# Attention inside a decoder step: scores of a head pair in two stretches, softmax blocks of both heads turned at one step

## The chip, the cores and the metric

The kernel runs on 1 core of one Trainium2 chip. The metric is device time of one execution in microseconds (us); the median of 3 runs of the kernel before is 1062.48 us, the runs lie between 1062.13 and 1064.51 us.

## The reference, cut to what matters

The whole is one inference step of a two-layer decoder for a prompt of 512 tokens and 8 sample tokens. The change touches one part only: the prompt's attention in the even layer, 16 heads of 64 features.

```python
def dilated_attn_prompt(q, k, v, slopes):
    qf = q.astype(jnp.float32) * (Dh ** -0.5)
    ...
    for w, d in DIL_PATTERNS:                 # (128,1), (512,4), (2048,16)
        ...
        s = jnp.einsum('bnirhd,bnjrhd->bnrhij', qs, kk)
        bias = -slopes[:, None, None] * (dist * d).astype(jnp.float32)
        s = jnp.where(valid[None, :, None, None], s + bias, -jnp.inf)
        m = jnp.max(s, axis=-1, keepdims=True)
        p = jnp.exp(s - m)
        l = jnp.sum(p, axis=-1)
        o = jnp.einsum('bnrhij,bnjrhd->bnirhd', p, vv) / l
        ...
    return combine_patterns(outs, lses)
```

For 512 tokens the three patterns and their merging come to one causal softmax per head, with a bias table that holds the slopes and the logarithm of how many patterns see a pair of positions. So a head is: scores of 512 queries against the keys up to each query, softmax, and the weighted sum of v.

## The kernel before, in words

**Products.** Nearly all of TensorE's work is products of a weight tile with the modulated input `h0` (1024 features by 520 tokens). Each operand is cut into a high part in the reduced format and a low part, the rest; a product is high times high, high times low, low times high. One product has 8 steps `k`, and a step is 6 matmuls (3 pairs of operands, each in two halves of 256 and 264 columns), written by `mm3` into a tile `mm`. ScalarE (ACT) makes the high part of the weights of a later product (`w_hi`, tile `whi`), VectorE (DVE) the low part in two pieces (`w_lo`, tile `wlo`).

**Head pairs.** `head_pair(p)`, for p from 0 to 7, handles two heads: four products, v, k, gate and q. After each, ACT copies the product out of PSUM (the PSUM side memory of TensorE), and then `sample_z` has DVE copy the 8 sample columns of the same tile into `zs`. The attention work of pair p itself is laid between the product steps of the next pair (of the next stage for p = 7).

**Steps and queues.** What is laid between is set by `tick()`, called once behind every product step. `at(n, f)` runs f at n ticks from now, ahead of all else; `put(f, after=n)` runs f at the earliest n ticks from now, at most one such call per tick; `put_fill` fills ticks in which no `put` call is due; `put2` has a list of its own, served at even ticks. `Q0 = 5`: the ticks of the list in `head_pair` count from 5 ticks behind the q product. So the order on every engine is fixed when the program is written; each engine then works through its list in order and waits with semaphores.

**One pair's work.** `score(blocks)`: for each block of 128 queries 6 matmuls with 64 rows, the two heads in the upper and the lower half of the rows; blocks 0 and 1 together (256 columns each), block 2 (384 columns) and block 3 (512) apart. `soft`: DVE adds the bias and finds the minimum, ACT takes the exponential, `norm` scales. `turn(e, g)` (line 604) transposes the softmax blocks of head e in three groups g of 4, 3 and 3 blocks, into an `aux` tile; ACT copies it to a high part, DVE makes the low part one tick later (`lo_of`, line 146 as a helper's line). `v_out` (line 518) transposes v, ACT copies it twice (`vtm`, and the high part in tile `v`), DVE makes its low part. `weigh(e, jb)`, four for each head, is two matmuls with `v`, the high part first and then the low part; `weigh(0, 2)` is the first that uses group 2 of head 0. `q_rows` transposes the q columns of the samples (line 536). The sample tokens' own window scores (`window_scores`, `window_sums`) are four DVE instructions of 1.2 us for each pair. `ada_two` and `ada_two_fin` prepare the next layer's modulation after every second pair: 32 matmuls, then 4 transposes with a reduction and three small instructions on DVE. The `aux` tiles share four PSUM buffers, taken in turn.

Of the kernel before, what the change touches and what calls it, by code (L numbers as in the profile page):

```python
# [18 lines left out]
P = 128  # L19
D = 1024  # L20
KT = D // P
S = 512
NB = 8
T = S + NB
# [62 lines left out]
def hybrid_kernel(ctx: ExitStack, tc: tile.TileContext, a, o):  # L87
# [17 lines left out]
    def tt(n=T, dt=F32, p=P):  # L105
        n_made[0] += 1
        return tp.tile([p, 530], dt, name=f"t_{n_made[0]}", tag="t")[:, 0:n]
# [14 lines left out]
    def aux(shape):  # L122
        return mk(auxp, shape, F32, "aux")
# [60 lines left out]
    def at(dt, fn, *args):  # L184
        seqn[0] += 1
        heapq.heappush(timed, (now[0] + dt, seqn[0], fn, args))
# [5 lines left out]
    def put_fill(fn, *args, after=0):  # L192
        fill.append((now[0] + after, fn, args))
# [314 lines left out]
    qdr = dram.tile([KT, NB, P], F32, name="qdr")  # L508

    Q0 = 5  # L510

    def head_pair(p):
        st = {}

        def v_out(vf):
            pt = aux([P, 4, P])
            for i in range(4):
                nc.tensor.transpose(pt[:, i, :], vf[:, i * P:(i + 1) * P], ident)  # L518
            vtm = tt(S)
            act(vtm, flat(pt))  # L520
            at(1, load, wv[:, :, p * P:(p + 1) * P], p4(vtm))
            vhl = t4(dt=F32R).rearrange("p (a e l d) -> p a e l d", a=4, e=2, l=2)
            vte = vtm.rearrange("p (a e d) -> p a e d", a=4, e=2)
            act(vhl[:, :, :, 0, :], vte)
            at(2, lo_of, vhl[:, :, :, 1, :], vte, vhl[:, :, :, 0, :])
            st["v"] = vhl
# [15 lines left out]
        def window_load():  # L542
            kw = big().rearrange("p (t b d) -> p t b d", t=2, b=NB)
            c = a["cache_win_k"][0].rearrange("b s h d -> s b (h d)")[:, :, p * P:(p + 1) * P]
            load(kw[:, 0], c[896:1024])
            load(kw[0:96, 1], c[512:896].rearrange("(n s) b d -> n s b d", s=4)[:, 0])
            load(kw[96:128, 1], c[0:512].rearrange("(n s) b d -> n s b d", s=16)[:, 0])
            st["kw"] = kw
            ada_w[p] = ada_load(1, "ss", p)
            if p % 2:  # L550
                at(20, put_fill, ada_two, 1, "ss", p - 1, (ada_w[p - 1], ada_w[p]))

        def q_load():
            st["qb"] = t4().rearrange("p (b d) -> p b d", b=NB)
# [3 lines left out]

        def score(blocks):

            ss_ = [aux([P, S]) for _ in range(2)]
            for qb in blocks:
                N = max(H0, (qb + 1) * P)
                c0 = H0 if qb == 1 else 0
                for c, (x, y) in enumerate(((0, 0), (0, 1), (1, 0))):
                    for e in range(2):
                        r = slice(64 * e, 64 * e + 64)
                        mm(
                            ss_[e][:, c0:c0 + N], st["q"][x][r, qb * P:(qb + 1) * P], st["k"][y][r, 0:N],
                            c == 0, c == 2,  # L570
                        )
            for i, qb in enumerate(blocks):
                for e in range(2):
                    soft(e, qb, ss_[e][:, i * H0:])

        def soft(e, qb, s):
            if qb == 0:
                st["mn", e], st["ls", e] = mk(cp, [P, 4], F32, "mn", 4), mk(cp, [P, 4], F32, "ls", 4)
                st["E", e] = []
            n = (qb + 1) * P  # L580
            mn, ls = st["mn", e][:, qb:qb + 1], st["ls", e][:, qb:qb + 1]
            sb = tt(n)
            nc.vector.tensor_tensor_reduce(  # L583
                out=sb, in0=s[:, 0:n], in1=bt[e][:, S - n:S], scale=1.0, scalar=3e38, op0=ALU.add, op1=ALU.min,
                accum_out=mn,
            )
            st["E", e].append(sb)
            at(1, act, sb, sb, ACTF.Exp, mn, -1.0, ls)
            at(3, norm, e, qb)
# [8 lines left out]

        groups = (((0, 0), (1, 0), (2, 0), (3, 0)), ((1, 1), (2, 1), (3, 1)), ((3, 3), (2, 2), (3, 2)))

        def turn(e, g):
            ep = aux([P, S])
            for c, blk in enumerate(groups[g]):
                nc.tensor.transpose(ep[:, c * P:(c + 1) * P], st["E", e][blk[0]][:, blk[1] * P:(blk[1] + 1) * P], ident)  # L604
            n = len(groups[g]) * P
            if g < 2:
                st["T", e, g] = hilo_later(1, ep[:, 0:n], n)
            else:
                st["T", e, g] = hi, lo = T2[e]
                act(hi[:, P:S], ep[:, 0:n])  # L610
                at(1, lo_of, lo[:, P:S], ep[:, 0:n], hi[:, P:S])

        def weigh(e, jb):
            if jb == 0:
# [31 lines left out]
        vf = tt(S)  # L646
        act(p2(vf), vps[:, :, 0:H0])
        sample_z(0, 48 + p, vps)
        put_fill(v_out, vf, after=2)
        kps = ps01[1] if p == 0 else z_tile(0, 40 + p, h0)  # L650
        kf = tt(S)
        act(p2(kf), kps[:, :, 0:H0])
# [19 lines left out]
            sample_z(0, 32 + p, qps)  # L672

        at(1, q_lo)
        for blocks, n in (((0, 1), 0), ((2,), 3), ((3,), 5)):
            put(score, blocks, after=Q0 + n)
        for e, fn, ticks in (
            (0, turn, (11, 13, 15)), (1, turn, (12, 14, 17)), (0, weigh, (18, 19, 20, 21)), (1, weigh, (22, 23, 24, 26)),
        ):
            for i, n in enumerate(ticks):  # L680
                put(fn, e, i, after=Q0 + n)
        put_fill(q_rows, after=4)


    T2 = [(tr(S), tr(S)) for _ in range(2)]
# [743 lines left out]
```

## Time and profile before

| | |
|---|---|
| median of 3 runs | 1062.48 us |
| the profiled execution, its own time | 1062.29 us |
| its span | 1060.3 us |
| TensorE (PE) busy | 98% |
| VectorE (DVE) busy | 59% |
| ScalarE (ACT) busy | 46% |
| attention stage of the head pairs, about | 60 to 322 us |

The time of an execution is 2.0 us longer than its span, so what the span gains or loses is read as a change of the time. PE's matmuls are pipelined: busy time overlaps, so what a piece of work costs is read here from the starts of the instructions around it and not from busy times. Column 2 of a timeline row is the busy time of the row's instructions; where several like instructions are merged, the row gives their count.

### The profile page before, as it was taken

How to read it: one execution, taken by the hardware profiler on the slowest of the kernel's cores; microseconds unless marked ns; L12 is line 12 of the kernel's file. 1: busy time of each engine (PE TensorE's matmuls, PEld its weight loads, DVE VectorE, ACT ScalarE, POOL GpSimd, SP SyncE). 2: the span in 40 equal slices, each digit the busy share in tenths (PEclk: the TensorE clock that was granted, in tenths of full speed). 3: DMA queues.
4: the chain of work that ended last, by engine and by line, in shares of the span. 5: the costliest groups of instructions: out<-in, count | busy, mean ns of one | idle time of the engine just before them, and what ended most of it. 6: DMA issues, size and time to landing. Idle time of an engine off the chain costs nothing.

```text
span 1060.3 us, 21050 instructions
## 1 busy us (share of the span) xinstructions
PE 1036.2 (98%) x8682; PEld 991.1 (93%) x8682; DVE 623.1 (59%) x1470; ACT 489.1 (46%) x884; POOL 4.3 (0%) x33
## 2 busy tenths in 40 slices
PE   5999999999999999999999999999999999999996
PEld 3899999999989999999999998999999999999996
DVE  4666676766785444456344486665657576674443
ACT  5666567665654222224233474435444453333333
POOL 0000000000000000000000000000000000000000
PEclk9999999999999999999999999999999999999999
DMA  9576654666536636613744246363826423225322
GB/s 348 209 255 196 184 157 169 173 211 190 142 119 203 196 107 194 199 60 129 240 154 140 100 159 205 103 204 118 261 83 213 159 80 129 80 83 169 100 71 81
DMA packets 82175, 168.95 MB, mean 159 GB/s; under 512 B 7208, under 2 KB 47240, under 8 KB 79000
## 3 DMA queue, kind: packets, MB, share of 16 engines
q1 hardware_dynamic: 81792, 167.09, 48.9%
q8 instruction: 68, 1.11, 0.4%
q10 hardware_dynamic: 288, 0.52, 0.1%
q14 instruction: 27, 0.22, 0.1%
HBM read 149.40 MB, written 18.65 MB: 158 GB/s over the span
## 4 chain that ended last, share of the span: by engine, by line
PE 90%; DVE 5%; ACT 2%; issue 1%; DVEq 0%; ACTq 0%
PE mm L160 74%; PE aux L160 13%; DVE t L146 2%; PE aux L604 1%; ACT t L140 1%; DVE wlo L146 1%; DVE t L149 0%; PE aux L1299 0%; PE aux L518 0%; DVE big L149 0%; PE aux L973 0%; PE aux L980 0%; PE aux L374 0%; ACT md L140 0%; ACT whi L140 0%
## 5 line engine op out<-in xcount | busy, mean ns | idle before, releaser
L160 PE MATMUL mm<-t,whi 128*128 128x256 f32 (+1 forms) x4608 | 759.1, 286 | 1.1 <-DVE zs L143 0.8
L160 PEld LDWEIGHTS mm<-t,whi 128*128 128x128 f32 x4608 | 636.1, 188 | 19.9 <-issue 15.5
L160 PE MATMUL mm<-t,wlo 128*128 128x256 f32 (+2 forms) x2304 | 465.8, 282 | 0.0
L160 PEld LDWEIGHTS mm<-t,wlo 128*128 128x128 f32 x2304 | 358.1, 188 | 0.0
L146 DVE TENSOR_TENSOR wlo<-wraw,whi 128x512 fp32r<-128x512 f32 x288 | 188.4, 683 | 58.1 <-ACT whi L140 57.4
L140 ACT ACTIVATE whi<-wraw 128x1024 fp32r<-128x1024 f32 x144 | 151.6, 1053 | 94.3 <-PE mm L160 58.7
L146 DVE TENSOR_TENSOR t<-t,t 128x520 fp32r<-128x520 f32 (+6 forms) x182 | 119.0, 657 | 99.3 <-ACT t L140 97.7
L140 ACT ACTIVATE t<-t 128x520 fp32r<-128x520 f32 (+3 forms) x116 | 71.0, 616 | 161.8 <-DVE t L149 103.1
L140 ACT ACTIVATE t<-aux 128x512 f32<-128x512 f32 (+7 forms) x156 | 70.9, 464 | 133.3 <-PE aux L160 83.4
L140 ACT ACTIVATE t<-mm 128x512 f32<-128x512 f32 (+2 forms) x116 | 56.3, 507 | 111.3 <-PE mm L160 109.1
L146 DVE TENSOR_TENSOR t<-aux,t 128x384 fp32r<-128x384 f32 (+6 forms) x120 | 58.6, 494 | 42.8 <-ACT t L140 38.0
L160 PE MATMUL aux<-t,t 64*128 64x256 f32 (+6 forms) x384 | 54.0, 324 | 0.0
L160 PE MATMUL aux<-t,v 128*128 128x512 f32 (+2 forms) x224 | 50.0, 325 | 0.0
L160 PEld LDWEIGHTS aux<-t,t 64*128 64x128 f32 (+1 forms) x384 | 41.0, 186 | 4.3
L583 DVE CUSTOM_DVE_ANT_0 t<-aux,t 128x128 f32<-128x128 f32 (+3 forms) x64 | 28.2, 488 | 27.5 <-PE aux L160 27.5
L140 ACT ACT_TABLE_LOAD x32 | 41.1, 1283 | 1.3 <-PEq L1414 0.7
L140 ACT ACTIVATE t<-t,mn 128x128 f32<-128x128 f32 (+3 forms) x64 | 35.4, 554 | 7.9 <-DVE mn L583 7.9
L160 PEld LDWEIGHTS aux<-t,v 128*128 128x128 f32 x224 | 34.8, 188 | 1.8 <-DVE t L146 0.8
L149 DVE SCALAR_TENSOR_TENSOR big<-v,ksc,big 128x256 f32<-128x256 f32 x64 | 27.7, 480 | 11.8 <-ACT big L140 10.4
L143 DVE COPY zs<-mm 128x8 f32<-128x8 f32 x76 | 12.0, 158 | 37.2 <-ACT t L140 31.8
L146 DVE TENSOR_TENSOR t<-mm,t 128x512 f32<-128x512 f32 (+1 forms) x24 | 16.5, 689 | 29.2 <-PE mm L160 21.6
L146 DVE TENSOR_TENSOR gtmp<-mm,mG 128x8 f32<-128x8 f32 x16 | 2.6, 165 | 44.8 <-PE mm L160 44.8
(153 smaller groups left out, 557.7 us busy)
## 6 DMA issues: line engine op xcount, KB each, us to landing
wraw<-in_w_in_e SPq DMA_DIRECT2D x64, 512.0 KB, 4.9
wraw<-in_w_in_o SPq DMA_DIRECT2D x48, 512.0 KB, 3.7
big<-in_ada_e SPq DMA_DIRECT2D x12, 1024.0 KB, 11.8
big<-in_ada_o SPq DMA_DIRECT2D x12, 1024.0 KB, 9.8
wraw<-in_w_out_e SPq DMA_DIRECT2D x16, 512.0 KB, 3.9
big<-in_state_ret SPq DMA_DIRECT2D x16, 512.0 KB, 8.0
out_new_ret_sample<-big SPq DMA_DIRECT2D x16, 512.0 KB, 5.1
wraw<-in_w_out_o SPq DMA_DIRECT2D x16, 512.0 KB, 3.4
```

What stands on the lines that cost most here:

```text
L140: return nc.scalar.activation(out=out, in_=in_, func=func, scale=scale, **kw)
L143: return nc.vector.tensor_copy(out, in_)
L146: return nc.vector.tensor_tensor(out=out, in0=in0, in1=in1, op=op)
L149: return nc.vector.scalar_tensor_tensor(out=out, in0=in0, scalar=scalar, in1=in1, op0=op0, op1=op1)
L160: nc.tensor.matmul(out, lhsT=lhsT, rhs=rhs, start=start, stop=stop)
L583: nc.vector.tensor_tensor_reduce(out=sb, in0=s[:, 0:n], in1=bt[e][:, S - n:S], scale=1.0, scalar=3e38, op0=ALU.add, op1=ALU.min, accum_out=mn,
L604: nc.tensor.transpose(ep[:, c * P:(c + 1) * P], st["E", e][blk[0]][:, blk[1] * P:(blk[1] + 1) * P], ident)
```

## The change

The scores of blocks 2 and 3 form one stretch at tick Q0 + 4 (before: block 2 at Q0 + 3, block 3 at Q0 + 5), in four `aux` tiles, where block 2's two and block 3's two were asked for apart before. `q_rows` is called at the head of the first stretch of scores. `turns(g)` transposes group g of both heads at one tick (before: six `turn` calls at six ticks); the low part of head 1 is asked for two ticks later. The transposes of the next pair's v stand in `turns(0)`, behind those of the two heads, and their copies behind the heads' copies (before: a fill some 4 ticks earlier). In the last pair `ada_two` is asked for 28 ticks behind, and not 20.

```diff
         def v_out(vf):
             pt = aux([P, 4, P])
             for i in range(4):
                 nc.tensor.transpose(pt[:, i, :], vf[:, i * P:(i + 1) * P], ident)
+            return lambda: v_rows(pt)
+
+        def v_rows(pt):
             vtm = tt(S)
             act(vtm, flat(pt))
...
-                at(20, put_fill, ada_two, 1, "ss", p - 1, (ada_w[p - 1], ada_w[p]))
+                at(20 if p < KT - 1 else 28, put_fill, ada_two, 1, "ss", p - 1, (ada_w[p - 1], ada_w[p]))
...
-            ss_ = [aux([P, S]) for _ in range(2)]
+            if blocks[0] == 0:
+                q_rows()
+                pair = [aux([P, S]) for _ in range(2)]
+                out = {(e, qb): pair[e][:, qb * H0:] for e in range(2) for qb in blocks}
+            else:
+                out = {(e, qb): aux([P, S]) for qb in blocks for e in range(2)}
             for qb in blocks:
                 N = max(H0, (qb + 1) * P)
-                c0 = H0 if qb == 1 else 0
                 for c, (x, y) in enumerate(((0, 0), (0, 1), (1, 0))):
                     for e in range(2):
                         r = slice(64 * e, 64 * e + 64)
                         mm(
-                            ss_[e][:, c0:c0 + N], st["q"][x][r, qb * P:(qb + 1) * P], st["k"][y][r, 0:N],
+                            out[e, qb][:, 0:N], st["q"][x][r, qb * P:(qb + 1) * P], st["k"][y][r, 0:N],
                             c == 0, c == 2,
                         )
...
-        def turn(e, g):
-            ep = aux([P, S])
-            for c, blk in enumerate(groups[g]):
-                nc.tensor.transpose(ep[:, c * P:(c + 1) * P], st["E", e][blk[0]][:, blk[1] * P:(blk[1] + 1) * P], ident)
+        def turns(g):
+
             n = len(groups[g]) * P
-            if g < 2:
-                st["T", e, g] = hilo_later(1, ep[:, 0:n], n)
-            else:
-                st["T", e, g] = hi, lo = T2[e]
-                act(hi[:, P:S], ep[:, 0:n])
-                at(1, lo_of, lo[:, P:S], ep[:, 0:n], hi[:, P:S])
+            eps_ = [aux([P, S]) for _ in range(2)]
+            for e in range(2):
+                for c, blk in enumerate(groups[g]):
+                    nc.tensor.transpose(
+                        eps_[e][:, c * P:(c + 1) * P], st["E", e][blk[0]][:, blk[1] * P:(blk[1] + 1) * P], ident
+                    )
+            later = v_next.pop()() if g == 0 and v_next else None
+            for e in range(2):
+                ep = eps_[e]
+                if g < 2:
+                    st["T", e, g] = hilo_later(1 + e, ep[:, 0:n], n)
+                else:
+                    st["T", e, g] = hi, lo = T2[e]
+                    act(hi[:, P:S], ep[:, 0:n])
+                    at(1 + e, lo_of, lo[:, P:S], ep[:, 0:n], hi[:, P:S])
+            if later is not None:
+                later()
...
-        put_fill(v_out, vf, after=2)
+        if p:
+            v_next.append(lambda: v_out(vf))
+        else:
+            put_fill(lambda: v_out(vf)(), after=2)
...
-        for blocks, n in (((0, 1), 0), ((2,), 3), ((3,), 5)):
+        for blocks, n in (((0, 1), 0), ((2, 3), 4)):
             put(score, blocks, after=Q0 + n)
-        for e, fn, ticks in (
-            (0, turn, (11, 13, 15)), (1, turn, (12, 14, 17)), (0, weigh, (18, 19, 20, 21)), (1, weigh, (22, 23, 24, 26)),
-        ):
+        for g, n in enumerate((11, 13, 16)):
+            put(turns, g, after=Q0 + n)
+        for e, ticks in ((0, (18, 19, 20, 21)), (1, (22, 23, 24, 26))):
             for i, n in enumerate(ticks):
-                put(fn, e, i, after=Q0 + n)
-        put_fill(q_rows, after=4)
+                put(weigh, e, i, after=Q0 + n)
```

On ACT, around the turning of pair 0's blocks, the program of before has these rows. `v_880` is the high part of v, `t_857` and `t_859` are softmax blocks being scaled, `aux_923` and `aux_945` hold the turned group 0 of head 0 and head 1, `mm_832` is the next pair's k product.

```order
L140 ACTIVATE v_880<-t_878 128x8x64
L140 ACTIVATE t_857<-t_857,ls_770 128x512
L140 ACTIVATE t_859<-t_859,ls_774 128x512
L140 ACTIVATE t_928<-aux_923 128x512
L140 ACTIVATE t_932<-mm_832 128x512
L140 ACTIVATE t_950<-aux_945 128x512
L140 ACTIVATE whi_959<-wraw_707 128x1024
```

At the same place the changed program has the following, where `aux_912` and `aux_913` are group 0 of the two heads, `aux_922` is the next pair's v turned, and `mm_818` is the k product.

```order
L140 ACTIVATE t_849<-t_849,ls_773 128x512
L140 ACTIVATE t_927<-aux_912 128x512
L140 ACTIVATE t_930<-aux_913 128x512
L140 ACTIVATE t_933<-aux_922 128x512
L140 ACTIVATE v_935<-t_933 128x8x64
L140 ACTIVATE t_938<-mm_818 128x512
L140 ACTIVATE whi_958<-wraw_707 128x1024
```

The copy of the k product stood second behind the scaling, with one turned tile ahead of it; now it stands fifth, with two turned tiles and both copies of v ahead.

On DVE, from the copy of the k product's sample columns (`zs_94<-mm_832`) to the low part of group 2 of head 0 (`t_545`), the program of before reads as follows. `t_929`, `t_951`, `t_967` and `t_986` are the low parts of groups 0 and 1, `big_681` is the sample window, `wlo` the low part of weights, `t_977` that of k.

```order
L143 COPY zs_94<-mm_832 128x8
L146 TENSOR_TENSOR t_929<-aux_923,t_928 128x512
L639 TENSOR_REDUCE t_542<-big_681 128x8x2
L146 TENSOR_TENSOR t_951<-aux_945,t_950 128x512
L146 TENSOR_TENSOR big_681<-big_681,v_807 128x1024
L146 TENSOR_TENSOR t_967<-aux_962,t_966 128x384
L639 TENSOR_REDUCE t_542<-big_681 128x8x2
L146 TENSOR_TENSOR wlo_994<-wraw_707,whi_959 128x512
L146 TENSOR_TENSOR t_986<-aux_981,t_985 128x384
L146 TENSOR_TENSOR wlo_994<-wraw_707,whi_959 128x512
L146 TENSOR_TENSOR t_977<-t_932,t_976 128x512
L146 TENSOR_TENSOR t_545<-aux_997,t_544 128x384
```

The changed program, first from the copy on:

```order
L143 COPY zs_94<-mm_818 128x8
L146 TENSOR_TENSOR t_928<-aux_912,t_927 128x512
L656 TENSOR_REDUCE t_542<-big_681 128x8x2
L146 TENSOR_TENSOR t_931<-aux_913,t_930 128x512
L146 TENSOR_TENSOR v_935<-t_933,v_935 128x8x64
L146 TENSOR_TENSOR t_971<-aux_962,t_970 128x384
```

and then directly on to the same low part:

```order
L146 TENSOR_TENSOR wlo_992<-wraw_707,whi_958 128x512
L146 TENSOR_TENSOR t_974<-aux_963,t_973 128x384
L146 TENSOR_TENSOR big_681<-big_681,v_825 128x1024
L146 TENSOR_TENSOR wlo_992<-wraw_707,whi_958 128x512
L146 TENSOR_TENSOR t_983<-t_938,t_982 128x512
L656 TENSOR_REDUCE t_542<-big_681 128x8x2
L146 TENSOR_TENSOR t_545<-aux_1005,t_544 128x384
```

The same twelve instructions stand between the copy and `t_545` inclusive, in another order, with one more among them: the low part of v, `v_935`.

## Rows read from the trace of the kernel before

**Rows 1.** The page, its group of the copies of sample columns (busy us, mean ns of one | idle us of DVE just before them, and what ended most of it), and one stretch of the head pairs and one around the last pair from the view of stretches (busy us and count of instructions of PE, weight loads, DVE, ACT and POOL, then the granted TensorE clock, the DMA share and GB/s).

```profile
L143 DVE COPY zs<-mm 128x8 f32<-128x8 f32 x76 | 12.0, 158 | 37.2 <-ACT t L140 31.8
...
60.00:80.00 20.00, 20.00 (x170) 18.78 (x168) 14.63 (x42) 15.42 (x35) 0.00 (x0) 1.00 0.70 241
300.00:320.00 20.00, 19.00 (x171) 17.69 (x171) 15.93 (x31) 7.53 (x12) 0.40 (x3) 1.00 0.20 62
```

**Rows 2.** The timeline of PE in pair 0: start in us, busy us, engine, line, operation, tiles and count. Rows of `mm<-t,whi` begin a product step; `aux<-csm,zs` is `q_rows`, `aux<-t,t` are scores, L518 is v, L604 are turned softmax blocks.

```profile
61.24 0.27 PE L536 MATMUL aux<-csm,zs 128*8 128x128 f32 x1
...
61.84 0.40 PE L160 MATMUL mm<-t,wlo 128*128 128x256 f32 x2
62.16 0.98 PE L160 MATMUL aux<-t,t 64*128 64x256 f32 x12
...
63.90 0.64 PE L160 MATMUL mm<-t,whi 128*128 128x256 f32 x4
...
65.09 0.40 PE L160 MATMUL mm<-t,wlo 128*128 128x256 f32 x2
65.43 0.79 PE L160 MATMUL aux<-t,t 64*128 64x384 f32 x6
...
66.95 0.64 PE L160 MATMUL mm<-t,whi 128*128 128x256 f32 x4
...
67.77 0.97 PE L160 MATMUL aux<-t,t 64*128 64x512 f32 x6
...
69.50 0.60 PE L518 MATMUL aux<-csm,t 128*128 128x128 f32 x4
...
70.42 0.40 PE L160 MATMUL mm<-t,wlo 128*128 128x256 f32 x2
70.66 0.64 PE L160 MATMUL mm<-t,whi 128*128 128x256 f32 x4
71.13 0.41 PE L160 MATMUL mm<-t,wlo 128*128 128x256 f32 x2
71.38 0.64 PE L160 MATMUL mm<-t,whi 128*128 128x256 f32 x4
...
75.86 0.49 PE L604 MATMUL aux<-csm,t 128*128 128x128 f32 x3
...
76.91 0.49 PE L604 MATMUL aux<-csm,t 128*128 128x128 f32 x3
```

**Rows 3.** The same timeline, pair 0: the turning of group 0 of head 0, and `weigh(0, 2)` and `weigh(0, 3)` (two matmuls each, high part and then low part).

```profile
73.54 0.60 PE L604 MATMUL aux<-csm,t 128*128 128x128 f32 x4
...
83.04 0.65 PE L160 MATMUL aux<-t,v 128*128 128x256 f32 x2
...
84.25 0.40 PE L160 MATMUL aux<-t,v 128*128 128x256 f32 x2
```

**Rows 4.** The timeline of ACT at that place: the two copies of v, the copy of group 0 of head 0, the copy of the k product. In brackets the idle time before, and what ended it.

```profile
70.93 0.57 ACT L140 ACTIVATE t<-aux 128x512 f32<-128x512 f32 x1
71.54 0.63 ACT L140 ACTIVATE v<-t 128x512 fp32r<-128x512 f32 x1
...
74.17 0.60 ACT L140 ACTIVATE t<-aux 128x512 fp32r<-128x512 f32 x1 [0.39 <-PE aux L604]
74.67 0.59 ACT L140 ACTIVATE t<-mm 128x512 f32<-128x512 f32 x1
```

**Rows 5.** The timeline of DVE at that place: the low part of v and the instruction behind it, the copy of the k product's sample columns and the low part behind it, a low part of 384 columns by itself, and the low parts of group 2 of the two heads.

```profile
72.40 0.67 DVE L146 TENSOR_TENSOR v<-t,v 128x512 fp32r<-128x512 f32 x1
72.98 1.22 DVE L146 TENSOR_TENSOR big<-big,v 128x1024 f32<-128x1024 f32 x1
75.30 0.17 DVE L143 COPY zs<-mm 128x8 f32<-128x8 f32 x1 [1.09 <-PE aux L604]
75.38 0.68 DVE L146 TENSOR_TENSOR t<-aux,t 128x512 fp32r<-128x512 f32 x1
...
78.83 0.55 DVE L146 TENSOR_TENSOR t<-aux,t 128x384 fp32r<-128x384 f32 x1
...
82.70 1.01 DVE L146 TENSOR_TENSOR t<-aux,t 128x384 fp32r<-128x384 f32 x2
```

**Rows 6.** Pair 1: on DVE the copy of the sample columns and the low parts of group 2; on PE `weigh(0, 2)`; and, from the last pair, the DVE instructions of one `ada_two_fin`.

```profile
106.97 0.17 DVE L143 COPY zs<-mm 128x8 f32<-128x8 f32 x1 [1.07 <-PE aux L604]
...
114.37 1.01 DVE L146 TENSOR_TENSOR t<-aux,t 128x384 fp32r<-128x384 f32 x2
...
116.75 0.40 PE L160 MATMUL aux<-t,v 128*128 128x256 f32 x2
...
320.13 0.31 DVE L376 TENSOR_REDUCE m9x<-aux 128x36 f32<-128x144 f32 x1 [1.87 <-PE aux L374]
...
320.77 0.18 DVE L146 TENSOR_TENSOR mA<-m9x,pv 128x18 f32<-128x18 f32 x1
```

**Rows 7.** The last pair: on PE `ada_two` (32 matmuls, with its idle time before), the stretch behind the next product step, and `weigh(0, 2)`; on DVE the low parts of group 2.

```profile
308.34 1.93 PE L160 MATMUL aux<-big,scT 128*32 128x256 f32 x32 [1.00 <-DVE t L146]
...
311.04 0.49 PE L604 MATMUL aux<-csm,t 128*128 128x128 f32 x3
...
312.59 1.01 DVE L146 TENSOR_TENSOR t<-aux,t 128x384 fp32r<-128x384 f32 x2
...
314.35 0.40 PE L160 MATMUL aux<-t,v 128*128 128x256 f32 x2
```

More of the change, by code (lines that the diff above doesn't have):

```diff
@@ L510, in hybrid_kernel @@
     Q0 = 5
+    v_next = []
     def head_pair(p):
@@ L568, in score @@
                         mm(
-                            ss_[e][:, c0:c0 + N], st["q"][x][r, qb * P:(qb + 1) * P], st["k"][y][r, 0:N],
+                            out[e, qb][:, 0:N], st["q"][x][r, qb * P:(qb + 1) * P], st["k"][y][r, 0:N],
                             c == 0, c == 2,
                         )
-            for i, qb in enumerate(blocks):
+            for qb in blocks:
                 for e in range(2):
-                    soft(e, qb, ss_[e][:, i * H0:])
+                    soft(e, qb, out[e, qb])
         def soft(e, qb, s):
```

## The prediction

> **What bounds the kernel now.** I read the view of stretches first: in a stretch of the head pairs PE is busy for 20.00 of 20 us, at a granted clock of 1.00 (2.4 GHz), while DVE has 14.63 and ACT 15.42 [rows 1]. So there a microsecond of PE work taken away is a microsecond of time, as long as nothing that PE needs comes later than now; and DVE and ACT, a quarter idle on the mean, are the ones that could be late. Next the timeline of PE, for what each inserted stretch costs, and the timelines of ACT and DVE, for the place at which PE already waits. A plain product step lasts 0.72 us (70.66 to 71.38), and the next step normally begins 0.24 behind the last row of the one before (70.42 to 70.66) [rows 2].
>
> The place at which PE waits is `weigh(0, 2)`: from its start to that of `weigh(0, 3)` go 1.21 us, 0.49 without the plain step, where two such matmuls need 0.24 (2 times 0.12) [rows 2, 3]. The 0.25 is a wait for the second matmul's operand, the low part of group 2 of head 0. DVE starts it at 82.70 and, by the like row of 0.55, ends it at 83.25 [rows 5]; the second matmul was due at 83.04 + 0.12 = 83.16. So 0.09 too late costs PE 0.25: a wait costs its lateness and 0.16 more. This chain has no slack left.
>
> What sets that end? From the copy of the k product's sample columns at 75.30 to 83.25, 7.95 us, DVE goes from one instruction to the next; before the copy it stood idle for 1.09 [rows 5]. The row names a PE transpose as the releaser, but ACT's copy of the same product runs from 74.67 to 75.26 [rows 4], 0.04 ahead of the DVE copy, and the page's group says of these copies that they wait mostly for ACT [rows 1]. The low part behind the copy had its input at 74.17 + 0.60 = 74.77 [rows 4] and still started at 75.38 [rows 5]: what stands behind the copy on DVE waits with it. By the Trainium skill, "TensorE: Matmul & The Clock Gate", section on architectural detail, ScalarE and VectorE work through their queues strictly in order, and only PE pulls weight loads ahead; the trace agrees here.
>
> **The change, part by part.** *Scores.* From the start of a score stretch to the second step behind it go 1.74 us (12 matmuls of 256 columns), 1.52 (6 of 384) and 1.73 (6 of 512) [rows 2]; less a step 1.02, 0.80 and 1.01. The entry takes 0.34 and not 0.24 (65.09 to 65.43). So the stretches cost 1.12, 0.90 and 1.11. The two heads run side by side, so 384 to 512 is 128 columns more for three pairs of matmuls: 0.21, or 0.07 for each. Nine such units in the second stretch leave 0.27 that does not depend on size, twelve in the first leave 0.28. By the rate of the plain step (1560 columns in 0.72, 0.059 for 128) it would be 0.37 and 0.41. Joining two stretches saves that once: 0.27 to 0.41, and I take 0.35.
>
> The Trainium skill, "TensorEngine Tiling (Array Packing)", section on key properties, says that a change of tiling mode drains TensorE. It would put the fixed cost down to the 64-row mode, and by it alone the change is a gain of 8 times that.
>
> *Transposes.* Four cost 1.16 - 0.72 = 0.44, three 1.05 - 0.72 = 0.33 [rows 2]: 0.11 each with nothing left over. Joining six stretches of turns to three, and v's to the first, so saves next to nothing: I take 0.03 for a pair (0 to 0.05). *`q_rows`* costs 0.13: the high rows behind it take 0.60 to the next row and not 0.47 [rows 2]. Ahead of a score stretch it may cost anything from 0.02 to 0.13; I take a saving of 0.05. Together 0.43 a pair, 3.4 us for eight pairs, if nothing waits.
>
> *What stands in the way.* At the tick of the first turn ACT now has two turned tiles and both copies of v ahead of its copy of the k product, where it had one turned tile. Take pair 0. The turns start 0.85 earlier than 73.54 (0.35, 0.05, v's 0.44 that move into the turn, 0.01): 72.69. ACT's first copy starts 0.63 behind that, as now (73.54 to 74.17), at 73.32. Turned tiles follow each other at 0.50 (74.17 to 74.67), the first copy of v takes 0.61 (70.93 to 71.54), the second 0.53 (0.63 less the 0.10 by which ACT's starts overlap) [rows 3, 4]. So the k product's copy starts at 73.32 + 0.50 + 0.50 + 0.61 + 0.53 = 75.46, and not at 74.67: 0.79 later, and with it the DVE copy, at 76.09. Behind it stand the same instructions as now (7.95) and v's low part, 0.58 (72.40 to 72.98), which DVE did so far while it had time. The low part of group 2 ends at 84.62. PE is due at 83.16 - 0.43 = 82.73. It is 1.89 late, which costs 2.05. Pair 0 nets -0.43 - 0.25 + 2.05 = +1.37, and the even pairs alike: 4 times, 5.5 us.
>
> In pairs 1, 3 and 5 `ada_two` gives DVE time: there its chain, equally long (106.97 to 114.37 + 0.55), ends 1.95 before PE's 116.87 [rows 6]. The change eats that up: copy at 107.76, 7.95, v's 0.58, and the four instructions of `ada_two_fin`, which now fall ahead of the place, 0.74 (320.13 to 320.77 and 0.10): 117.03. PE is due at 116.87 - 0.43 + 0.44 (those transposes) = 116.88. It costs 0.15 + 0.16 = 0.31; net -0.12, three times -0.4. This is the least certain term: 0 to 0.8 of wait.
>
> In the last pair `ada_two` waits 1.00 us for a buffer [rows 7]; asked for later, it waits no longer, and its own 2.08 (308.34 to 311.04 less a step, and 0.10 of entry) moves behind `weigh(0, 2)`. But that was time for DVE: its low part ends at 312.59 + 0.55 = 313.14, less 0.41 = 312.73, with no v to turn; PE comes at 314.35 + 0.12 - 0.43 - 1.00 - 2.08 = 310.96. Late by 1.77, cost 1.93, net -0.43 - 1.00 + 1.93 = +0.5.
>
> Sum: 5.5 - 0.4 + 0.5 = +5.6 us on the profiled execution's 1062.29 (median 1062.48): **1067.9 us**, 0.5% slower.
>
> Edits at no cost: the four `aux` tiles of blocks 2 and 3 need those of blocks 0 and 1 free again, which were asked for four steps (2.9 us) ahead; without that cover PE would wait there too. v's low part was free, as DVE's idle 1.09 hid it; that cover is what goes.
>
> **The rivals.** *Only the gains show (faster).* If ACT and DVE catch up before `weigh(0, 2)`, PE loses 8 times 0.43, 4 times 0.25 and the last pair's 1.00: 5.4 us, 1056.9. For it: DVE's idle quarter [rows 1], and the rule on draining. Against: the chain from the copy on has no idle time in it. It decides whether the low part comes 1.9 us earlier than I reckon, at the place `weigh(0, 2)` of the even pairs. Chance 0.06. *Half of it (same).* If the even pairs' wait is about 0.7 instead of 2.05, gains and waits cancel: 1062.3; chance 0.06. *Later still.* The low parts of weights queue on DVE behind the same chain; were they late by 1 us for each pair's next product, it would be 8 us more, 1076. Against: they are made a product ahead, over 5 us. Chance 0.02. *The clock falls.* A PE wait of 2 us is longer than any in this stage now; in the stretch with the 1.00 us wait the granted clock stayed 1.00 [rows 1]. If it went to 1.2 GHz for two steps behind each of five long waits, 10 steps cost 0.72 more each: 1075. The Trainium skill, the same clock page, says that an idle TensorE is throttled down; no row here shows it. Chance 0.03.
>
> **How the numbers follow.** My forecast has 0.83. Its own range: with savings at their upper bound (0.41 + 0.05 + 0.11), no wait in the odd pairs and a shorter last one, 3 to 4 us slower; with savings of 0.3, even pairs at 1.6, odd ones at +0.4 and the last at +1.0, 8.6 slower. That gives 1065.2 to 1071.0, beyond which some 0.05 of the forecast's chance and the rivals lie. About 0.2% (2.1 us) is what a measurement of this kernel can tell from no change. Faster 0.06, same 0.06, slower 0.88.
>
> **What would show it.** In the trace after: PE idle before the second matmul of `weigh(0, 2)`, about 1.9 us in even pairs and the last, ended by DVE, and 0 to 0.6 in pairs 1, 3, 5; the DVE copy of sample columns behind ACT's fifth copy, idle for about 3 us before it; no wait of `ada_two` in the last pair; one score stretch of 12 matmuls some 0.35 cheaper than two; transposes still 0.11 each. I am wrong if PE shows no idle time there, or if the copy does not wait for ACT.

## The result, and the profile after

The changed kernel takes 1068.13 us (median of 6 runs, 1066.78 to 1069.47); the kernel before, on the same chip, 1062.39 us (6 runs, 1061.70 to 1064.51). The ratio is 1.005, 95% interval 1.004 to 1.006: slower, by 5.7 us where 5.6 were forecast. The profiled execution took 1068.70 us, its span 1066.7.

Of the 6.4 us between the spans of the two traces, 5.97 arise between 58 and 346 us. The starts of every 192nd product matmul (a pair has four products of 48), set against each other in the two timelines, say what was lost between them; the pair named is the one whose attention lies there:

| pair | 0 | 1 | 2 | 3 | 4 | 5 | 6 | 7 | sum |
|---|---|---|---|---|---|---|---|---|---|
| after less before, us | +1.45 | +0.02 | +1.44 | -0.17 | +1.51 | -0.12 | +1.36 | +0.48 | +5.97 |
| forecast, us | +1.37 | -0.12 | +1.37 | -0.12 | +1.37 | -0.12 | +1.37 | +0.5 | +5.6 |

Two groups from the page of after (columns as in [rows 1]):

```profile
L160 PE MATMUL aux<-t,v 128*128 128x512 f32 (+2 forms) x224 | 51.2, 327 | 8.7 <-DVE t L146 8.6
...
L143 DVE COPY zs<-mm 128x8 f32<-128x8 f32 x76 | 12.0, 158 | 56.5 <-ACT t L140 56.5
```

DVE now idles 56.5 us before its copies of sample columns, 37.2 before [rows 1], all of it put down to ACT. And PE waits 8.6 us in the `weigh` matmuls for DVE's low parts. The timeline of PE in pair 0 of after (start, busy; L540 is `q_rows`, L615 the turns, L519 v):

```profile
61.77 0.27 PE L540 MATMUL aux<-csm,zs 128*8 128x128 f32 x1
61.97 0.99 PE L160 MATMUL aux<-t,t 64*128 64x256 f32 x12
...
63.71 0.64 PE L160 MATMUL mm<-t,whi 128*128 128x256 f32 x4
...
65.63 0.40 PE L160 MATMUL mm<-t,wlo 128*128 128x256 f32 x2
65.96 1.50 PE L160 MATMUL aux<-t,t 64*128 64x384 f32 x12
...
68.22 0.65 PE L160 MATMUL mm<-t,whi 128*128 128x256 f32 x4
...
72.55 1.03 PE L615 MATMUL aux<-csm,t 128*128 128x128 f32 x8
73.42 0.60 PE L519 MATMUL aux<-csm,t 128*128 128x128 f32 x4
...
74.58 0.64 PE L160 MATMUL mm<-t,whi 128*128 128x256 f32 x4
...
82.56 0.28 PE L160 MATMUL aux<-t,v 128*128 128x256 f32 x1
84.55 0.39 PE L160 MATMUL aux<-t,v 128*128 128x256 f32 x1 [1.71 <-DVE t L146]
84.78 0.64 PE L160 MATMUL mm<-t,whi 128*128 128x256 f32 x4
```

The last three rows are `weigh(0, 2)`: its second matmul starts 1.99 us behind the first, where 0.12 is normal, so 1.87 of waiting, and the step behind it another 0.23, not 0.12. The same place in ACT's timeline, and in DVE's:

```profile
73.19 1.58 ACT L140 ACTIVATE t<-aux 128x512 fp32r<-128x512 f32 x3 [0.91 <-PE aux L615]
74.79 0.63 ACT L140 ACTIVATE v<-t 128x512 fp32r<-128x512 f32 x1
75.33 0.58 ACT L140 ACTIVATE t<-mm 128x512 f32<-128x512 f32 x1
```

```profile
73.22 1.23 DVE L146 TENSOR_TENSOR big<-big,v 128x1024 f32<-128x1024 f32 x1 [1.67 <-DMA v<-qdr]
75.94 0.17 DVE L143 COPY zs<-mm 128x8 f32<-128x8 f32 x1 [1.49 <-ACT t L140]
...
82.82 1.21 DVE L656 TENSOR_REDUCE t<-big 128x16 f32<-128x1024 f32 x1
83.95 1.01 DVE L146 TENSOR_TENSOR t<-aux,t 128x384 fp32r<-128x384 f32 x2
```

Two turned tiles and the first copy of v stand merged in ACT's row of 73.19, then v's second copy, then the k product's at 75.33 (74.67 in [rows 4]). The DVE copy follows at 75.94 (75.30 in [rows 5]), and from there DVE goes without a pause to the low part of group 2, which by the like row of 0.55 ends at 84.50. PE was due at 82.56 + 0.12.

The last pair, where neither a k product nor a v stands in the way, has the same wait (PE, then DVE):

```profile
316.09 0.28 PE L160 MATMUL aux<-t,v 128*128 128x256 f32 x1
318.08 0.39 PE L160 MATMUL aux<-t,v 128*128 128x256 f32 x1 [1.71 <-DVE t L146]
```

```profile
316.34 1.21 DVE L656 TENSOR_REDUCE t<-big 128x16 f32<-128x1024 f32 x1
317.47 1.01 DVE L146 TENSOR_TENSOR t<-aux,t 128x384 fp32r<-128x384 f32 x2
```

And the granted clock in stretches with such a wait (columns as in [rows 1]):

```profile
80.00:100.00 20.00, 18.29 (x151) 17.37 (x152) 12.62 (x33) 9.88 (x21) 0.00 (x0) 1.00 0.73 211
300.00:320.00 20.00, 18.29 (x151) 17.52 (x150) 17.78 (x41) 11.21 (x23) 0.40 (x3) 1.00 0.26 86
```

PE is busy 1.71 us less than the stretch, and the clock stays 1.00.

### The profile page after: what moved, and what is told of

Its sections match the earlier page's. It is cut to its first block, busy times and chain, and to the rows that moved or that the text cites. A ratio compares the mean times of both kernels' runs of the same rounds, so it can differ in the third digit from the quotient of the medians.

```text
span 1066.7 us, 21054 instructions
## 1 busy us (share of the span) xinstructions
PE 1034.8 (97%) x8682; PEld 991.0 (93%) x8682; DVE 623.7 (58%) x1470; ACT 485.8 (46%) x884; POOL 4.3 (0%) x33
## 3 DMA queue, kind: packets, MB, share of 16 engines
q8 instruction: 68, 1.11, 0.4%
## 4 chain that ended last, share of the span: by engine, by line
PE 85%; DVE 9%; ACT 3%; issue 1%; DVEq 0%; ACTq 0%
PE mm L160 71%; PE aux L160 12%; DVE t L146 4%; ACT t L140 2%; DVE wlo L146 1%; DVE t L656 1%; PE aux L615 1%; DVE big L146 1%; DVE t L149 0%; PE aux L1318 0%; DVE v L146 0%; ACT v L140 0%; DVE big L149 0%; PE aux L999 0%; PE aux L992 0%
## 5 line engine op out<-in xcount | busy, mean ns | idle before, releaser
L140 ACT ACTIVATE t<-aux 128x384 fp32r<-128x384 f32 (+7 forms) x156 | 67.9, 465 | 144.1 <-PE aux L160 86.9
L143 DVE COPY zs<-mm 128x8 f32<-128x8 f32 x76 | 12.0, 158 | 56.5 <-ACT t L140 56.5
```

The source lines that it names most:

```text
L140: return nc.scalar.activation(out=out, in_=in_, func=func, scale=scale, **kw)
L143: return nc.vector.tensor_copy(out, in_)
```

## The experiments

All are edits of the changed kernel. "Wait" is the start of the second matmul of `weigh(0, 2)` less that of the first, less 0.12, in each one's trace, as a mean over pairs 0, 2, 4, 6 (even), over 1, 3, 5 (odd), and in the last pair. "Stage" is the change against before between 58 and 346 us, from starts of product matmuls as above; medians carry the rest of the program too, which varies by some 1 to 2 us between executions.

| kernel | even | odd | last | stage | median (ratio to before, 95%) |
|---|---|---|---|---|---|
| before | 0.14 | 0 | 0 | 0 | 1062.4 |
| after | 1.87 | 0.21 | 1.87 | +5.97 | 1068.13 (1.004 to 1.006) |
| e1 v's copies later | 0.81 | 0.19 | 1.89 | +3.49 | 1065.70 (1.0018 to 1.0042) |
| e2 k's sample columns later | 0.38 | 0.25 | 1.84 | -0.30 | 1061.83 (0.9989 to 1.0007) |
| e3 v's low part later | 1.26 | 0.18 | 1.87 | +3.55 | 1067.11 (1.0025 to 1.0053) |
| e4 six turns again | 0 | 0 | 0.26 | -4.40 | 1058.25 (0.9948 to 0.9973) |
| e5 v turned alone | 0.64 | 0.18 | 1.84 | +0.74 | 1063.77 (1.0004 to 1.0023) |
| e6 scores apart | 1.38 | 0.18 | 0.81 | +9.06 | 1070.96 (1.0068 to 1.0093) |
| e7 v's low part twice | 2.51 | 0.94 | 1.85 | +15.55 | 1074.95 (1.0094 to 1.0125) |
| e8 last `ada_two` at 20 | 1.88 | 0.21 | 0.11 | +5.51 | 1068.59 (1.0041 to 1.0069) |
| e9 second reduction later | 0.74 | 0 | 0.75 | -0.62 | 1061.56 (0.9983 to 1.0002) |
| e10 e2 and e9 | 0 | 0 | 0.71 | -4.43 | 1058.09 (0.9946 to 0.9974) |

**e1: v's copies on ACT behind the k product's.**

```diff
-                later()
+                at(1, later)
```

> Edit: in the changed kernel ACT's two copies of the turned v come one tick later, so behind its copy of the k product and not ahead of it; PE's program stays. Theory (the DVE chain that stands behind the copy of the k product's sample columns, and is held by ACT's order, makes PE wait in `weigh(0, 2)`): that DVE copy comes 0.61 + 0.53 = 1.14 us earlier, PE's wait in the even pairs shrinks from about 1.87 to about 0.75, in pairs 1, 3, 5 from 0.2 to nothing, in the last pair (no v, no k) it stays 1.87. Time 4 x 1.1 + 3 x 0.2 = 5.0 below 1068.1, about 1063. Rival A (the turning of both heads at one step makes PE late by itself, whatever ACT's order): wait unchanged, 1068. Rival B (only v's low part, newly in DVE's list, makes it too long): nothing leaves that list, so the wait stays within 0.2 of 1.87, 1067 to 1068.

The wait of the even pairs fell by 1.06, as the theory had it, and they came out 1.16 shorter than in after on the mean. Rivals A and B fall. But the sum stayed at 2.5 of the 5.0: the odd pairs kept their 0.19, and the last pair lost 2.2 more than in after. There `weigh(0, 0)` waited as well (0.42 before it and 0.11 inside), the wait of 1.89 followed, and behind that the granted clock fell (PE, then the view of stretches; the product step at 314.77 lasts 1.14, where 0.72 is normal):

```profile
314.55 0.39 PE L160 MATMUL aux<-t,v 128*128 128x256 f32 x1 [1.74 <-DVE t L146]
314.77 0.90 PE L160 MATMUL mm<-t,whi 128*128 128x256 f32 x4
315.47 0.64 PE L160 MATMUL mm<-t,wlo 128*128 128x256 f32 x2
315.91 0.63 PE L160 MATMUL aux<-t,v 128*128 128x256 f32 x2
```

```profile
312.00:318.00 6.00, 4.26 (x23) 4.02 (x22) 4.43 (x9) 1.06 (x2) 0.10 (x1) 0.75 0.26 90
```

DVE was later there because ACT was. Ahead of pair 7's first exponential (`t<-t,mn`) ACT's timeline has a row `ACT_TABLE_LOAD`, 1.28 us long. In e1 it began only when DVE's minimum `mn` was there, in after ahead of it; DVE wrote that minimum from 293.11 on in e1, from 297.32 on in after (ACT, e1 and then after):

```profile
293.26 1.28 ACT L140 ACT_TABLE_LOAD   x1 [1.00 <-DVE mn L591]
294.55 0.40 ACT L140 ACTIVATE t<-t,mn 128x128 f32<-128x128 f32 x1
```

```profile
296.49 1.28 ACT L140 ACT_TABLE_LOAD   x1
297.78 0.40 ACT L140 ACTIVATE t<-t,mn 128x128 f32<-128x128 f32 x1
```

So the exponential came 1.44 us behind that and not 0.46, and what DVE does behind it came 0.98 later. In pair 6 the same row stands behind the same wait in e1, e3 and e7, without a longer wait in `weigh(0, 2)` than in the other even pairs. Why it stands ahead of the wait in one trace and behind it in another is not shown; the theory of e1 does not touch it. Over pairs 0 to 6 alone e1 gained 4.7 us.

**e2: DVE's copy of k's sample columns later.**

```diff
-        sample_z(0, 40 + p, kps)
+        at(4, sample_z, 0, 40 + p, kps)
```

> Edit: in the changed kernel DVE's copy of the k product's 8 sample columns (0.1 us) is asked for 4 ticks later; ACT and PE keep their programs, and DVE has the same work. Theory: the chain no longer stands behind ACT's fifth copy; the low part of group 0 starts when ACT's first turned tile is done, some 2 us earlier, so PE's wait in the even pairs falls from 1.87 to below 0.5 and in pairs 1, 3, 5 to nothing; the last pair has no k product and stays at 1.87. Time 4 x 1.5 + 3 x 0.2 = 6.6 below 1068.1, about 1061.5, so at or below the kernel before. Rival A (the joined turns by themselves): wait unchanged, 1068. Rival B (v's low part in DVE's list): that stays, wait at least 1.3, 1066 to 1068.

An instruction of 0.16 us, moved behind others on the same engine, took 6.3 us off and brought the kernel back to the time of before. This settles that what stands behind the copy was held by it. 0.38 remained in the even pairs, within what was expected, and 0.25 in the odd ones, where I had expected nothing; the last pair did not move. The list had another part: in pair 0 it now pauses once more for ACT, and from there on DVE goes without a pause to the low part at 81.44.

```profile
76.36 0.56 DVE L146 TENSOR_TENSOR t<-aux,t 128x384 fp32r<-128x384 f32 x1 [0.44 <-ACT t L140]
```

**e3: v's low part out of the list.**

```diff
-            at(2, lo_of, vhl[:, :, :, 1, :], vte, vhl[:, :, :, 0, :])
+            at(12, lo_of, vhl[:, :, :, 1, :], vte, vhl[:, :, :, 0, :])
```

> Edit: in the changed kernel v's low part on DVE is asked for 12 ticks later and not 2, which takes it out of the list between the copy of sample columns and the low part of group 2. Theory: the list is 0.58 us shorter, so PE's wait in the even pairs falls from 1.87 to about 1.3, in pairs 1, 3, 5 from 0.2 to nothing. Time 4 x 0.58 + 3 x 0.2 = 2.9 below 1068.1, about 1065.2. Rival B (that low part alone is what was added to a list without slack, and the copies' order on ACT adds nothing): the wait falls to the 0.13 of the kernel before, 4 x 1.7 + 0.6 less, 1060.5. Rival A (the joined turns): 1068.

The wait of the even pairs fell by 0.61, the length of that instruction, and no more: it is one part, not the cause. The odd pairs kept 0.18, where nothing was expected. The stage gained 2.4; the median fell by 1.0 only. The profiled execution had lost 2.4 us before 58 us; where the others lost time is not on record. With e1 the account of the even pairs is 1.06 for ACT's order, 0.61 for DVE's list, and 0.2 for the rest of 1.87.

**e4: six turns again, v alone, scores still joined.**

```diff
...
-        for g, n in enumerate((11, 13, 16)):
-            put(turns, g, after=Q0 + n)
-        for e, ticks in ((0, (18, 19, 20, 21)), (1, (22, 23, 24, 26))):
+        for e, fn, ticks in (
+            (0, turn, (11, 13, 15)), (1, turn, (12, 14, 17)), (0, weigh, (18, 19, 20, 21)), (1, weigh, (22, 23, 24, 26)),
+        ):
             for i, n in enumerate(ticks):
-                put(weigh, e, i, after=Q0 + n)
+                put(fn, e, i, after=Q0 + n)
```

> Edit: the changed kernel with the turning undone: six turns at six ticks and v turned alone as a fill, as before; scores in two stretches, q_rows beside them and the last pair's later ada_two stay. Theory: the waits came with the turns and v, the gain with the scores: 8 x 0.39 for the scores and 0.1 for q_rows, no wait of 1.00 of ada_two in the last pair but about 0.7 in `weigh(0, 2)` for it, and the 0.13 to 0.25 of the four even pairs about as before: 3 to 4.5 below the kernel before, 1058 to 1059.5. Rival (blocks 2 and 3 in one stretch are what makes DVE and ACT late, as they get both blocks of both heads at once): the waits of 1.87 stay in the even pairs, 1066 to 1068.

0.4% faster than before. The scores' part of the change is a gain; the turns' part is what costs. And the last pair's wait, which had no k and no v to blame, was 0.26 and not the 0.7 I gave it. What differs stands in DVE's timeline, in pair 0 of e4 and then of e2:

```profile
80.61 0.55 DVE L146 TENSOR_TENSOR t<-aux,t 128x384 fp32r<-128x384 f32 x1
81.08 1.21 DVE L647 TENSOR_REDUCE t<-big 128x16 f32<-128x1024 f32 x1
```

```profile
80.31 1.21 DVE L656 TENSOR_REDUCE t<-big 128x16 f32<-128x1024 f32 x1
81.44 1.01 DVE L146 TENSOR_TENSOR t<-aux,t 128x384 fp32r<-128x384 f32 x2
```

With six turns and the scores in two stretches the low part of group 2 of head 0 stands ahead of the second window reduction; with joined turns behind it; in the last pair likewise (low part at 306.72 and reduction at 307.19 in e4, reduction at 309.15 and low part at 310.28 in e2). (In before, with the scores in three, it stood behind it too, as the rows of the order show, and the even pairs waited their 0.14.)

**e5: v turned alone, turns of both heads still joined.**

```diff
-        if p:
-            v_next.append(lambda: v_out(vf))
-        else:
-            put_fill(lambda: v_out(vf)(), after=2)
+        put_fill(lambda: v_out(vf)(), after=2)
```

> Edit: in the changed kernel the next pair's v is turned alone again, as a fill some 4 ticks earlier, with its copies and its low part; the joined turns and scores stay. Theory (two things lengthen the way to the low part of group 2: v's two copies ahead of the k product's on ACT, which the run with the copies one tick later priced at 1.99 - 0.95 = 1.04 us, and v's low part on DVE, which the run with that part later priced at 1.99 - 1.39 = 0.60): both go, so PE's wait in the even pairs falls from 1.87 to 0.2 to 0.7 (the second turned tile stays ahead of the k product's copy), in pairs 1, 3, 5 to nothing; the last pair stays at 1.87. Time 4 x 1.2 to 1.65 and 0.6 below 1068.1: 1061 to 1063. Rival A (the joined turns by themselves make the wait): even pairs stay above 1.3, 1066 or more.

The wait fell to 0.64, inside what was expected; the odd pairs kept 0.18, and the time is 0.8 above the range. So v accounts for 1.23 of the 1.87: 1.06 on ACT and 0.61 on DVE by e1 and e3, less the 0.44 of its transposes, which gave that much time between turn and `weigh` and now come earlier. The other 0.64 is no matter of v.

**e6: scores in three stretches, turns joined.**

```diff
-                q_rows()
...
-        for blocks, n in (((0, 1), 0), ((2, 3), 4)):
+        for blocks, n in (((0, 1), 0), ((2,), 3), ((3,), 5)):
...
+        put_fill(q_rows, after=4)
```

> Edit: in the changed kernel the scores are in three stretches again and q_rows is a fill, as before; the turns and v stay joined. Theory (the gain of the joined scores, 8 x 0.39, is there in full, and stands beside the waits): without it 3.1 us above 1068.1, about 1071, with PE's waits in the even pairs and the last at 1.5 to 2.2. Rival (PE, which arrives earlier by the joined scores, only waits longer for it, so the gain is lost in the waits of five pairs): without them those waits fall by 0.39 each, 8 x 0.39 - 5 x 0.39 = 1.2 above, 1069.3.

2.8 above after: the gain of the scores and `q_rows` is not swallowed by the waits. The wait in the even pairs only spread, 1.38 at `weigh(0, 2)` and 0.49 at `weigh(0, 0)`, together the same 1.87; in the last pair likewise, 0.81 and 1.03.

**e7: v's low part made twice.**

```diff
-            at(2, lo_of, vhl[:, :, :, 1, :], vte, vhl[:, :, :, 0, :])
+            for _ in range(2):
+                at(2, lo_of, vhl[:, :, :, 1, :], vte, vhl[:, :, :, 0, :])
```

> Edit: in the changed kernel v's low part is made twice on DVE, one directly behind the other (0.58 us more of DVE's time in each pair, the result is the same). Theory (the list behind the copy of sample columns has no slack in any pair but the last): PE's wait grows by 0.58 in the even pairs to about 2.45, and in pairs 1, 3, 5 from 0.2 to 0.8; the last pair has no v and stays. 4 x 0.58 + 3 x 0.58 = 4.1 above 1068.1, about 1072. Rival (DVE, a quarter idle on the mean, has room for it): 1068. If the granted clock falls behind a wait, as it did once behind 0.42 and 1.89 us of waiting within 3 us, up to 2 us more for each place.

The waits grew by 0.64 and 0.73, and the time by 6.8, not 4.1. Most of the rest is the clock. In pair 0, PE's rows at `weigh(0, 2)` and the stretch around them; in pair 6 the stretch with a wait nearly as long (2.49):

```profile
84.54 0.58 PE L160 MATMUL aux<-t,v 128*128 128x256 f32 x1 [2.35 <-DVE t L146]
84.92 1.07 PE L160 MATMUL mm<-t,whi 128*128 128x256 f32 x4
...
86.22 0.63 PE L160 MATMUL aux<-t,v 128*128 128x256 f32 x2
```

```profile
86.00:92.00 6.00, 6.00 (x42) 5.91 (x42) 1.88 (x3) 0.60 (x1) 0.00 (x0) 0.85 0.96 204
...
291.00:297.00 6.00, 3.67 (x29) 3.37 (x28) 4.47 (x9) 2.03 (x3) 0.00 (x0) 1.00 0.59 184
```

From step to `weigh` 1.30 instead of 0.72 in pair 0, at matmuls 0.21 to 0.22 apart instead of 0.12; the same in pairs 2 and 4, not in pair 6. Pairs 0, 2 and 4 lost 3.58, 3.68 and 3.62 us, pair 6 2.18: some 1.4 for each fall of the clock. The stage of the profiled execution (1076.76 us, where the median is 1074.95) lost 9.6 more than that of after: 2.6 and 2.2 from the longer waits, most of the rest from the three falls. What spared pair 6 is not shown.

**e8: the last pair's `ada_two` at 20 ticks, as before.**

```diff
-                at(20 if p < KT - 1 else 28, put_fill, ada_two, 1, "ss", p - 1, (ada_w[p - 1], ada_w[p]))
+                at(20 if p < KT - 1 else 20, put_fill, ada_two, 1, "ss", p - 1, (ada_w[p - 1], ada_w[p]))
```

> Edit: in the changed kernel ada_two of the last pair is asked for at 20 ticks, as before. Theory (those 32 matmuls, 2.08 us, and their wait for a buffer are time for DVE ahead of `weigh(0, 2)`): the wait of 1.87 there goes, and ada_two waits for a buffer again, about 1.0 to 1.4: 0.5 to 0.9 below 1068.1, 1067.2 to 1067.6. Rival (the low part of group 2 is late in the last pair whatever stands ahead of it on PE): the wait of 1.87 stays and that of ada_two is added, 1069.

The wait at `weigh(0, 2)` was gone (0.11) and `ada_two` did not wait for a buffer either: the pair was 1.7 shorter than in after. But then, at 337 to 340 us, PE waited for DVE, where after has no wait, and 1.2 of it was lost again (the first wait is for what DVE makes of an exponential):

```profile
337.39 0.44 PE L753 MATMUL aux<-csm,t 128*128 128x128 f32 x2 [0.61 <-DVE t L153]
...
339.57 0.43 PE L160 MATMUL aux<-pnr,csm 128*128 128x64 f32 x2 [0.31 <-DVE pnr L153]
```

That exponential came late by ACT, as in e1's last pair: the row `ACT_TABLE_LOAD` ahead of it stands behind the wait for DVE's maximum `sm` in e8, and ahead of it in after (ACT, e8 and then after):

```profile
334.85 1.28 ACT L140 ACT_TABLE_LOAD   x1 [2.20 <-DVE sm L742]
336.14 0.51 ACT L140 ACTIVATE t<-t,sm 128x257 f32<-128x257 f32 x1
```

```profile
333.93 1.28 ACT L140 ACT_TABLE_LOAD   x1
336.07 0.51 ACT L140 ACTIVATE t<-t,sm 128x257 f32<-128x257 f32 x1 [0.86 <-DVE sm L742]
```

DVE had `sm` ready at 334.77 in e8 and at 336.04 in after, so the exponential came 1.37 behind it and not 0.03. The time is that of after, but what the last pair gained was lost at another place, by a row that the edit does not name; no run has the edit without that.

**e9: the second window reduction two ticks later.**

```diff
-            at(1, window_sums, t, kw)
+            at(1 if t == 0 else 3, window_sums, t, kw)
```

> Edit: in the changed kernel the second of a pair's two window reductions on DVE is asked for two ticks later, nothing else. Theory, widened by what the kernel with six turns shows (there the low part of group 2 at 80.61 stands ahead of that reduction at 81.08, while in the kernels with joined turns the reduction at 80.31 stands ahead of the low part at 81.44): it leaves the list, 81.44 - 80.31 = 1.13 us, so PE's wait at `weigh(0, 2)` falls in the even pairs from 1.87 to about 0.75, in pairs 1, 3, 5 to nothing, and in the last pair too, which none of the other edits touched, from 1.87 to about 0.75. 5 x 1.13 + 3 x 0.2 = 6.2 below 1068.1, about 1062. Rival (the low part is late because its turn comes a tick later than the turn alone did, whatever stands ahead on DVE): waits unchanged, 1068.

As expected in all three kinds of pairs: 0.74, 0 and 0.75. The last pair, which no edit of k or v had touched, moved by 1.12.

**e10: the edits of e2 and e9 together.**

> Edit: both, the copy of the k product's sample columns 4 ticks later and the second window reduction two ticks later, in the changed kernel with all its joins. Theory (list and order account for every wait): none is left in pairs 0 to 6, 0.75 in the last. From the 1061.8 with the copy alone go the 0.37 of four pairs, the 0.25 of three and 1.13 in the last, and 0.1 of extra for each wait that ends: 4 x 0.47 + 3 x 0.35 + 1.13 = 4.1, about 1057.8, so 0.4% faster than the kernel before, and about level with the six turns (1058.25). Rival (what is left with the copy alone is the turn's lateness itself): 1061.8.

1058.09, 0.4% faster than before, with the change's joins all in place. No wait is left in pairs 0 to 6 (PE's waits between 56 and 350 us: total, times, longest; the longest is that of the last pair, the other, 0.47, stands in the next stage, at a place where before and after wait as long):

```profile
PE aux L160 <- DVE t L146: 1.0, 2, 0.6
```

## Why the prediction was right

**The mechanism held, step by step.** The traces differ by -0.19 at the stage's start, so 0.19 is added to times of after here. Copy of the k product on ACT: 75.52, forecast 75.46. DVE's copy: 76.13, forecast 76.09; DVE's idle time ahead of it was 1.49 and not about 3 us, as the window product in between waited until 73.22 for its load. Its chain: 8.56 long, forecast 7.95 + 0.58. Low part ready: 84.69, forecast 84.62. PE due: 82.87, forecast 82.73. Late by 1.82 and not 1.89; 1.87 of wait and 0.11 in the step behind it are 1.98, again 0.16 more than the lateness; forecast 2.05. The even pairs came out at +1.36 to +1.51.

**Scores.** By the recipe of the prediction, the joined stretch costs 68.22 - 65.96 - 0.72, and 0.09 more of entry (65.96 - 65.63 less 0.24): 1.63. Apart they cost 0.90 + 1.11 [rows 2]. That is 0.38 saved, between the bounds, 0.03 above the value taken; e6 puts scores and `q_rows` together at 2.8 us of time. The Trainium skill, "TensorEngine Tiling (Array Packing)", key properties, which lets a change of tiling mode drain TensorE, agrees with the sign: one such change less for each pair, and the fixed cost went once.

**`q_rows`, the mis-sized term.** It and the first stretch cost 63.71 - 61.77 - 0.72 = 1.22, before 0.13 + 1.12 = 1.25 [rows 2]: 0.03, not 0.05, in eight pairs 0.2 us. **Transposes** as forecast: 12 cost 74.58 - 72.55 - 0.72 = 1.31, 0.11 each.

**Odd pairs** waited 0.18 to 0.26 and 0.11 in the step behind, together about 0.32, where 0.31 was reckoned; they netted -0.09 on the mean instead of -0.12. That the size came out is in part luck. In after the chain does run without a pause from the copy to the low part, as reckoned; but a second limit stands close behind, which the prediction did not have. Where the chain starts earlier or is shorter (e1, e2, e3, e5), DVE pauses in pair 1 for PE's transposes in `ada_two_fin` (line 374), and goes on from there without a pause; in e3:

```profile
113.56 0.56 DVE L146 TENSOR_TENSOR t<-aux,t 128x384 fp32r<-128x384 f32 x1 [0.20 <-ACT t L140]
114.30 0.31 DVE L376 TENSOR_REDUCE m9x<-aux 128x36 f32<-128x144 f32 x1 [0.17 <-PE aux L374]
...
119.64 1.01 DVE L146 TENSOR_TENSOR t<-aux,t 128x384 fp32r<-128x384 f32 x2
```

So the odd pairs kept 0.18 to 0.25 in all four, where the expectations said nothing would be left. e9 took it away, as its reduction lies in this last part.

**Last pair**: `ada_two` waits no longer, `weigh(0, 2)` waits 1.87 where it was to be late by 1.77; +0.48, forecast +0.5. That `ada_two` was time for DVE is right: with it back at its place (e8) the wait is 0.11, and the pair is 1.3 shorter than in before, where the gains without any wait came to 1.43.

**What it left out.** It took the 7.95 us behind the copy as one piece. None of the instructions in it is an input of the low part at its end (`t_545<-aux_1005,t_544`); two of them were moved, the copy itself, ahead of everything, and the window reduction, 1.13 just ahead of the end. The prediction's rival of only gains named the point from which it decides, a low part 1.9 us earlier, and gave it 0.06 since the chain has no idle time in it. In the changed kernel that is right; but a chain without idle time can still hold work that might stand behind its end. e10 moves two of them and lands at 1058.1, near the rival's 1056.9. The rival of late weights did not come: all of PE's waits for DVE in this stage of after are for operands of `aux` tiles.

**The clock.** The rival of a falling clock did not come true in the changed kernel: 1.00 behind waits of 1.87. It did at the next dose, behind three of the four waits of 2.5 in e7, at about the 1.4 us each (two steps at 0.72 more) reckoned for it. The Trainium skill, "TensorE: Matmul & The Clock Gate", part 1, on the clock gate, has the idle engine throttled; e7 and e1 agree, after does not come to it.

## What to carry to other kernels

Joining matmuls of one shape saves PE a fixed price each time, but joined producers also hand their copies to the next engine in one lump; look at what small instruction, queued behind that lump on the next engine, has the critical work behind it. When a chain without idle time ends at a wait of PE, list its instructions and ask of each whether the end needs it: moving two that it did not need, 0.16 and 1.21 us long, was worth 10 us here. And where a run's time is not what its edit explains, look in the trace for a place that the edit does not touch: in e1 and e8 one row of ACT, 1.28 us long, behind a wait instead of ahead of it, hid what the edit gained.

## What the runs showed of the hardware

- A wait of PE costs more than its length: behind each one of 0.13 to 1.9 us at `weigh(0, 2)` the next step began 0.22 to 0.23 after the last matmul, and not 0.12; behind the one of 0.11 in e8 it began after 0.12.
- The granted clock stayed at 1.00 behind waits of 1.87 us (five places in after), fell behind three of four waits of 2.5 us in e7, and behind one of 1.89 us in e1, some 2 us ahead of which PE had waited 0.42 and 0.11. Matmuls then started 0.21 to 0.22 us apart instead of 0.12, the lower of the clock's two levels, at some 1.4 us for each fall. So a wait that grows a little can cost twice.
- ACT's row `ACT_TABLE_LOAD` takes 1.28 us. Begun while ACT would have waited anyway it cost nothing that PE saw (the exponential 0.03 us behind its operand in after); begun behind the wait it delayed the exponential by 0.98 us in e1 and 1.34 in e8.
